# A softmax kernel's stores move from ACT's hardware DMA queue to Pool's software queue

## The chip, the cores and the metric

The kernel runs on one core of a Trainium2 chip. Five of its parts appear below: DVE (VectorE), ACT (ScalarE) and Pool (GpSimd) compute, SP (SyncE) here only issues transfers and waits, and 16 DMA engines move the data. A transfer is issued by an instruction on a queue; it has landed when its semaphore (the counter on which the engine waits) lets the waiting engine go on. "The last load landed" is read from the start of the DVE operation that waited for it. The metric is device time in microseconds (us) of one execution. The span in a profile runs from the first to the last instruction of the program and is about 1.8 us shorter than the device time (before: 316.0 against 317.86 us in the profiled execution).

## The reference

```python
def setup_inputs():
    batch, seq, dim = 32, 512, 1024
    return {"x": np.random.randn(batch, seq, dim).astype(np.float32), "temperature": 0.5}

def reference(x, temperature):
    scaled = x / temperature
    shifted = scaled - np.max(scaled, axis=-1, keepdims=True)
    exp_x = np.exp(shifted)
    return (exp_x / np.sum(exp_x, axis=-1, keepdims=True)).astype(np.float32)
```

That is 16384 rows of 1024 floats: 67.11 MB are read and 67.11 MB written.

## The kernel before

The rows are cut into 16 tiles of 128 partitions with 8 rows each (4 MB a tile, 32 KB a partition, in one piece in DRAM and in SBUF). Six tile buffers are in use. SP issues the loads. A tile is worked on in two groups of four rows: DVE takes the maximum, ACT the exponential with its sum, DVE divides in place. When both groups of a tile are divided, ACT issues the store, and the load into that buffer waits for the store to land.

```python
TILES = [[8]] * 16
BUFS = 6
GROUP = 4
# ... (cut)
    def load():
        i = len(tiles)
        if i < len(TILES):
            xt = data.tile([P, sum(TILES[i]), d], f32, name="xt")
            nc.sync.dma_start(out=xt, in_=dram(xf, i))
            tiles.append(xt)
# ... maximum(g): tensor_reduce over four rows, then bias = -scale * top; exponential(g): four activations (cut)
    def divide(g):
        # ... (cut)
        nc.vector.reciprocal(recip, sums)
        for b in range(k):
            nc.vector.tensor_scalar_mul(
                tiles[i][:, a + b, :], in0=tiles[i][:, a + b, :], scalar1=recip[:, b : b + 1]
            )

    def store(g):
        i, _, _, part = groups[g]
        if part:
            a, k = part
            nc.scalar.dma_start(out=dram(of, i)[:, a : a + k, :], in_=tiles[i][:, a : a + k, :])
            if a + k == sum(TILES[i]):
                load()

    with tc.manual_schedule():
        for _ in range(BUFS):
            load()
        for g in range(len(groups) + 1):
            if g < len(groups):
                maximum(g)
                exponential(g)
            if g > 0:
                divide(g - 1)
                store(g - 1)
```

In the profile, L61 is the load, L70 the maximum, L79 the exponential, L91 the reciprocal, L93 the divide, L101 the store and L147 the program's end.

## Time and profile before

| | before |
|---|---|
| time, median | 318.11 us (3 runs, 318.0 to 318.13) |
| DVE, ACT, Pool busy | 75%, 47%, 0% |
| bytes, mean rate over the span | 134.25 MB, 425 GB/s |
| store: issue to landing, median | 38.6 us |
| load: issue to landing, median | 50.2 us |

These lines are from the page of the kernel before: busy time by engine; the DMA queues (packets, MB, share of the 16 engines' span); three groups of instructions (after the bar: busy us and mean ns of one, then the idle time before them and what ended it); and the DMA issues (size, median us to landing).

```profile
DVE 235.5 (75%) x224; ACT 149.6 (47%) x257; POOL 0.2 (0%) x4
...
q1 hardware_dynamic: 2304, 67.11, 49.7%
q10 hardware_dynamic: 2304, 67.11, 49.2%
...
L79 ACT ACTIVATE xt<-xt,bias 128x1024 f32<-128x1024 f32 x128 | 145.4, 1137 | 136.8 <-DVE recip L91 119.4
L70 DVE TENSOR_REDUCE top<-xt 128x4 f32<-128x4096 f32 x32 | 141.3, 4416 | 62.6 <-DMA xt<-in_x_dram 62.6
L93 DVE TENSOR_SCALAR xt<-xt,recip 128x1024 f32<-128x1024 f32 x128 | 87.7, 749 | 1.1
...
xt<-in_x_dram SPq DMA_DIRECT2D x16, 4096.0 KB, 50.2
out_dram<-xt ACTq DMA_DIRECT2D x16, 4096.0 KB, 38.6
```

The two queues together hold the engines for 98.9% of the span. Two rows of the table of windows (stretch, its length, busy us by engine, clock, DMA share, GB/s) show the steady part:

```profile
core 0: us, DVE busy (x) ACT busy (x) POOL busy (x), PEclk, DMA share, GB/s
...
80.00:120.00 40.00, 31.40 (x32) 18.96 (x33) 0.00 (x0) 1.00 1.00 433
...
240.00:280.00 40.00, 29.46 (x28) 19.44 (x34) 0.00 (x0) 1.00 1.00 433
```

A DMA share of 1.00 at 433 GB/s means that there is nothing to gain in the steady part from starting a transfer earlier, and nothing to lose from starting it a little later while others are queued (delay_all below, with every store held up: 1.0018 of this kernel's time). The packet records say how much later: from the fourth store to the thirteenth, a store's first packet starts 18.1 to 19.0 us after its issue, about when the store before it has finished. So a store's start has some 18 us of room there. The last store has little: its first packet starts 1.0 us after its issue. This is the timeline of the tail (start us, duration us, engine, line, operation):

```profile
282.62 4.42 DVE L70 TENSOR_REDUCE top<-xt 128x4 f32<-128x4096 f32 x1 [4.50 <-DMA xt<-in_x_dram]
...
290.13 0.34 ACTq L101 DMA_DIRECT2D out_dram<-xt  x1
...
299.61 2.74 DVE L93 TENSOR_SCALAR xt<-xt,recip 128x1024 f32<-128x1024 f32 x4
302.38 0.34 ACTq L101 DMA_DIRECT2D out_dram<-xt  x1
```

The last load has landed at 282.62 us, and the last store is issued 19.8 us later.

### The profile page before, as it was taken

The numbers are of one execution on the slowest core, as the hardware profiler recorded it, in microseconds if no ns is written. First come the engines' busy times: TensorE is split into PE (matmuls) and PEld (weight loads), VectorE is DVE, ScalarE is ACT, GpSimd is POOL, SyncE is SP. The second block draws the span as 40 slices with busy tenths as digits, with TensorE's granted clock in tenths as the row PEclk, the third lists the DMA queues.
The fourth block names the chain that finished last, engine by engine and source line by source line (L and its number), as shares of the span: only waits on it lengthen the run. The fifth ranks groups of instructions, "written<-read, shape, count | busy, mean of one in ns | idle before, by whom it ended". The sixth has DMA issues, their size and how long they took to land.

```text
span 316.0 us, 620 instructions
## 1 busy us (share of the span) xinstructions
DVE 235.5 (75%) x224; ACT 149.6 (47%) x257; POOL 0.2 (0%) x4
## 2 busy tenths in 40 slices
DVE  0399999999689494994949859497693976949720
ACT  0176666666526255361554605546064560645500
POOL 0000000000000000000000000000000000000000
DMA  8999999999999999999999999999999999999996
GB/s 332 411 452 423 373 460 415 452 425 431 436 427 440 427 444 423 444 419 448 415 452 411 452 408 456 423 444 427 436 431 432 440 423 444 419 444 419 452 411 274
DMA packets 4612, 134.25 MB, mean 425 GB/s; under 512 B 512, under 2 KB 512, under 8 KB 512
## 3 DMA queue, kind: packets, MB, share of 16 engines
q1 hardware_dynamic: 2304, 67.11, 49.7%
q10 hardware_dynamic: 2304, 67.11, 49.2%
q14 instruction: 4, 0.03, 0.0%
HBM read 67.11 MB, written 67.11 MB: 425 GB/s over the span
## 4 chain that ended last, share of the span: by engine, by line
DVE 49%; DMA 32%; another core or an unknown queue 9%; ACT 5%; issue 1%; DVEq 0%; SPq 0%
DVE top L70 29%; DMA xt<-in_x_dram 20%; DVE xt L93 18%; DMA out_dram<-xt 12%; ACT xt L79 5%; DVE recip L91 1%; DVE bias L73 1%; DVEq L147 0%; SPq L61 0%
## 5 line engine op out<-in xcount | busy, mean ns | idle before, releaser
L79 ACT ACTIVATE xt<-xt,bias 128x1024 f32<-128x1024 f32 x128 | 145.4, 1137 | 136.8 <-DVE recip L91 119.4
L70 DVE TENSOR_REDUCE top<-xt 128x4 f32<-128x4096 f32 x32 | 141.3, 4416 | 62.6 <-DMA xt<-in_x_dram 62.6
L93 DVE TENSOR_SCALAR xt<-xt,recip 128x1024 f32<-128x1024 f32 x128 | 87.7, 749 | 1.1
L79 ACT ACTIVATION_READ_ACCUMULATOR xt<-xt,bias 128x1 f32 x128 | 23.9, 187 | 0.0
L79 ACT ACT_TABLE_LOAD x1 | 1.3, 1283 | 13.0 <-DMA xt<-in_x_dram 13.0
L91 DVE RECIPROCAL recip<-sums 128x4 f32<-128x4 f32 x32 | 5.5, 171 | 2.1 <-ACT xt L79 2.1
L73 DVE TENSOR_SCALAR bias<-top 128x4 f32<-128x4 f32 x32 | 5.4, 170 | 1.1
L133 POOL MEMSET const-bfloat16-1.0<- 128x1 bf16 x1 | 0.1, 101 | 0.0
L133 POOL MEMSET const-uint8-127<- 128x1 uint8 x1 | 0.1, 101 | 0.0
L133 POOL MEMSET const-float32-0.0<- 128x1 f32 x1 | 0.1, 98 | 0.2 <-issue 0.2
L133 POOL MEMSET const-float32-1.0<- 128x1 f32 x1 | 0.1, 98 | 0.0
## 6 DMA issues: line engine op xcount, KB each, us to landing
xt<-in_x_dram SPq DMA_DIRECT2D x16, 4096.0 KB, 50.2
out_dram<-xt ACTq DMA_DIRECT2D x16, 4096.0 KB, 38.6
```

The lines of the kernel that those rows point to most:

```text
L70: nc.vector.tensor_reduce(out=top, in_=tiles[i][:, a : a + k, :], axis=mybir.AxisListType.X, op=extreme)
L73: nc.vector.tensor_scalar_mul(bias, in0=top, scalar1=-scale)
L79: nc.scalar.activation(tiles[i][:, a + b, :], tiles[i][:, a + b, :], mybir.ActivationFunctionType.Exp, bias=bias[:, b : b + 1], scale=scal ...
L91: nc.vector.reciprocal(recip, sums)
L93: nc.vector.tensor_scalar_mul(tiles[i][:, a + b, :], in0=tiles[i][:, a + b, :], scalar1=recip[:, b : b + 1])
L133: nc = _bacc.Bacc("TRN2", target_bir_lowering=False, num_devices=1)
```

## The change

The intent: take the stores off ACT's queue and give them to Pool, which has nothing else to do, so that ACT only computes. The price is that Pool's stores go through a software queue (q0, software_dynamic on the page after); what this adds before a store's first packet I could only estimate.

```diff
         if part:
             a, k = part
-            nc.scalar.dma_start(out=dram(of, i)[:, a : a + k, :], in_=tiles[i][:, a : a + k, :])
+            nc.gpsimd.dma_start(out=dram(of, i)[:, a : a + k, :], in_=tiles[i][:, a : a + k, :])
             if a + k == sum(TILES[i]):
                 load()
```

## The prediction

> **What bounds the kernel now.** The 16 DMA engines. The page counts 134.25 MB at a mean 425 GB/s; a table of 40 us windows shows DMA share 1.00 and 431 to 433 GB/s from 40 to 280 us. 134.2 MB at 433 GB/s is 310 us of the 316.0 us span; the rest is start and end (data stops near 313.2 us). DVE is busy 75%, ACT 47%; the waits of DVE (62.6 us on loads) and of ACT (119.4 us) are slack. The chain of waits (49% DVE) misleads: in the steady part every DVE stretch follows a wait for a load.
>
> **What the change moves.** Sixteen 4096 KB stores leave ACT's queue for Pool's; bytes and the work of DVE and ACT are the same. Removed: 16 issues of 0.34 us from ACT's queue. In the timeline a store already issues 0.12 us after its last divide, between exponentials, and ACT waits for DVE anyway. Gain: 0.
>
> [...] But each store comes just after the four divides (2.74 us); then DVE runs a 4.41 us reduce[...], so I expect each store to start 1 to 3 us later at most. In the steady part this costs nothing: stores take 38.6 us to land at a 19.3 us period, so two are in flight, with two or three loads (50.2 us).
>
> **Where it can show: the tail.** The last load lands at 282.6 us. Its compute takes 19.8 us; the last store issues at 302.38. From 282.6 the engines still have about 13.2 MB (30.5 us) to move, so without the last store they would run dry about 1 us after its issue. Two outcomes:
>
> - Shares stay equal (or loads get more): the last store's later start shows, +0.5 to 2.5 us. About 319 to 320.5 us.
> - Stores get a larger share. [...] If a software store's descriptors form one packet per engine, each store (9.7 us alone at 433 GB/s) passes the loads, landing in 10 to 20 us. Stores then no longer queue; the last load lands later, at about 291 us, and the 19.8 us of compute plus a 9.7 us store stand behind it, with the engines idle about 10 us. Estimate: span about 325, time 324 to 328 us.
>
> No trace here shows the software queue's packets; I give the first outcome about 62%, the second 36%.
>
> **Prediction:** 320.5 us, range 317.6 to 328. Faster by over 2%: 0.01; within 2%: 0.65; slower: 0.34.
>
> **What would show it.** Right: DVE and ACT busy and means unchanged (TENSOR_REDUCE 4414, TENSOR_SCALAR 749 ns); the store's queue listed as software, same 67.11 MB; 433 GB/s in 40 to 280 us. First outcome: median store landing stays near 38 us, last load near 283 us. Second: store landing 10 to 20 us, load landing above 55 us, last reduce-wait ending near 290 us, holes in the DMA row in the last three slices.
>
> **What would make it wrong.** Packets in the thousands and a steady rate under 425 GB/s[...]: over 328. [...] A start or end cost of the software queue outside the span. Faster than 317 only if the rate rises above 433 GB/s.

## The result, and the profile after

| | before | after |
|---|---|---|
| time, median | 318.08 us (4 runs, 318.0 to 318.13) | 318.28 us (4 runs, 318.17 to 318.68) |
| ratio | | 1.0009, 95% interval 0.9991 to 1.0026: the same |
| store: issue to landing, median | 38.6 us | 38.4 us |
| last load landed, profiled execution | 282.62 us | 282.87 us |

Ratios here are the mean time of one kernel's fast runs over that of the other's in the same rounds, so they are not quite the ratio of the medians quoted.

From the page of the kernel after; Pool's store instruction is now counted as work of Pool:

```profile
DVE 235.5 (74%) x224; ACT 149.6 (47%) x257; POOL 8.8 (3%) x20
...
q1 hardware_dynamic: 2304, 67.11, 49.5%
q0 software_dynamic: 2304, 67.11, 49.1%
...
issue 89%; DMA 4%; POOL 2%; POOLq 0%
...
L70 DVE TENSOR_REDUCE top<-xt 128x4 f32<-128x4096 f32 x32 | 141.3, 4416 | 62.8 <-DMA xt<-in_x_dram 62.8
L93 DVE TENSOR_SCALAR xt<-xt,recip 128x1024 f32<-128x1024 f32 x128 | 87.7, 749 | 1.1
...
L101 POOL DMA_DIRECT2D out_dram<-xt x16 | 8.6, 540 | 294.4 <-DVE xt L93 294.4
...
xt<-in_x_dram SPq DMA_DIRECT2D x16, 4096.0 KB, 50.2
out_dram<-xt POOLq DMA_DIRECT2D x16, 4096.0 KB, 38.4
```

Three readings. First, the software queue has the same 2304 packets as the hardware queue (16 stores of 128 data packets and 16 closing ones). Second, DVE's and ACT's durations have not moved. Third, the chain of waits is of no use here: it followed Pool's own queue back and calls 89% of the span "issue" (time in which the engine waited for nothing that the profile shows). The steady part, in the same two windows:

```profile
80.00:120.00 40.00, 31.14 (x31) 18.56 (x33) 1.06 (x2) 1.00 1.00 433
...
240.00:280.00 40.00, 29.46 (x28) 19.03 (x33) 1.06 (x2) 1.00 1.00 433
```

The tail of the kernel after, as a timeline:

```profile
282.87 4.42 DVE L70 TENSOR_REDUCE top<-xt 128x4 f32<-128x4096 f32 x1 [4.48 <-DMA xt<-in_x_dram]
...
290.65 0.53 POOL L101 DMA_DIRECT2D out_dram<-xt  x1 [18.82 <-DVE xt L93]
...
299.86 2.74 DVE L93 TENSOR_SCALAR xt<-xt,recip 128x1024 f32<-128x1024 f32 x4
302.90 0.53 POOL L101 DMA_DIRECT2D out_dram<-xt  x1 [11.72 <-DVE xt L93]
```

The last divide ends at 302.60 us and Pool begins 0.30 us later; before, the last divide ended at 302.35 us and ACT issued 0.03 us later. So the issue is 0.27 us later. (My texts say 0.12 and 0.38 us; there I had counted from the start of the next DVE operation, which overlaps the divide's end. The difference is the same.) Pool's store instruction takes 0.53 us, ACT's issue took 0.34 us.

One thing did get longer, at the very end. These rows list the semaphore instructions of SP's queue on the program's last line, in the kernel before and then in the kernel after (count, duration ns, first and last start us):

```profile
L147 SPq EVENT_SEMAPHORE  x7: 17/28/28, 270.5 to 315.9; - x7
```

```profile
L147 SPq EVENT_SEMAPHORE  x11: 17/28/28, 315.5 to 316.8; - x11
```

Before the program ends, SP goes through a list of waits for DMA semaphores: five wait instructions before the change, nine after it (the other two instructions of each row come later). Single times here are from the trace's records. In the kernel before, the earlier stores' waits are done while the last store is still moving; the last of them passes at 315.20 us and SP goes on at 315.26 us. In the kernel after, the first wait in SP's list passes only at 315.46 us, when the last store has landed, and eight more wait instructions, by then fulfilled, follow at 0.06 us each, so SP goes on at 316.01 us. The order of the list costs here as much as its length: the wait that passes last stood at its end before and stands at its head now. From the last data packet to the span's end it is 1.19 us before and 1.85 us after.

### The profile page after: what moved, and what is told of

The parts are those of the page before. It is cut to its first block, busy times and chain, and to the rows that moved or that the text cites. A ratio compares the mean times of both kernels' runs of the same rounds, so it can differ in the third digit from the quotient of the medians.

```text
span 316.9 us, 639 instructions
## 1 busy us (share of the span) xinstructions
DVE 235.5 (74%) x224; ACT 149.6 (47%) x257; POOL 8.8 (3%) x20
## 3 DMA queue, kind: packets, MB, share of 16 engines
q1 hardware_dynamic: 2304, 67.11, 49.5%
q0 software_dynamic: 2304, 67.11, 49.1%
## 4 chain that ended last, share of the span: by engine, by line
issue 89%; DMA 4%; POOL 2%; POOLq 0%
DMA xt<-in_x_dram 4%; POOL out_dram L101 2%; POOLq L147 0%; POOLq L101 0%
## 5 line engine op out<-in xcount | busy, mean ns | idle before, releaser
L70 DVE TENSOR_REDUCE top<-xt 128x4 f32<-128x4096 f32 x32 | 141.3, 4416 | 62.8 <-DMA xt<-in_x_dram 62.8
L101 POOL DMA_DIRECT2D out_dram<-xt x16 | 8.6, 540 | 294.4 <-DVE xt L93 294.4
## 6 DMA issues: line engine op xcount, KB each, us to landing
out_dram<-xt POOLq DMA_DIRECT2D x16, 4096.0 KB, 38.4
```

The source lines that it names most:

```text
L70: nc.vector.tensor_reduce(out=top, in_=tiles[i][:, a : a + k, :], axis=mybir.AxisListType.X, op=extreme)
L101: nc.gpsimd.dma_start(out=dram(of, i)[:, a : a + k, :], in_=tiles[i][:, a : a + k, :])
```

## The experiments

Sixteen kernels were run. Times of the kernel before in the same rounds had medians of 317.90 to 318.06 us.

### What a store's later start costs when nothing hides it: b2_act and b2_pool

With two buffers, every load waits for a store, so a store's start is in the time.

```diff
-BUFS = 6
+BUFS = 2
```

> Two tile buffers instead of six, stores from ACT: each load waits for a store to land, so every microsecond of a store's start is in the time. Estimate about 500 us (16 periods of about 31.5 us: 7.5 us of compute, a store and a load of about 12 us each when alone). It is the control for b2_pool.

> Two tile buffers, stores from Pool. Theory A (a software store starts only some tenths of a us later, as the issue at +0.38 us after the divides against +0.12 us shows): 2 to 6 us longer than b2_act over 14 to 16 exposed stores. Theory B (my prediction's term: 1 to 3 us later start per store, which six buffers only hid): 14 to 45 us longer. Theory C (no cost at all): within 1 us.

Measured: 494.75 us (494.52 to 495.0) from ACT, 501.80 us (501.77 to 502.29) from Pool; both correct. Time from issue to landing, minimum/median/maximum, from ACT and then from Pool:

```profile
DMA to landing us min/median/max: 11.1/11.1/12.1
```

```profile
DMA to landing us min/median/max: 11.3/11.4/12.3
```

The last load's data ended at 460.34 us with ACT and at 467.35 us with Pool. Fourteen loads had waited for a store by then, so a software store costs 0.50 us each (7.01 us over 14): 0.27 us of it a later issue after the divide, 0.2 to 0.3 us more from issue to landing. The packet records agree: the first packet starts 0.84 us after the issuing instruction's start on ACT and 1.10 us on Pool. (The 0.50 us is from one trace of each. By the median times, less about 0.5 us of longer end, it is 0.4 to 0.5 us.) That is just above what theory A expected for the total (2 to 6 us, measured 7.05) and far below theory B, the 1 to 3 us of the prediction. Theory C falls too: the cost is real, and six buffers hide it.

### Holding the stores up on purpose: delay_all, delay_but_last, delay_last, delay_last_double

Pool first copies 3072 elements per partition of the tile, which takes 2.75 us, and then issues the store.

```diff
             a, k = part
+            if True:                       # delay_all
+            # delay_but_last: if i < len(TILES) - 1;  delay_last: if i == len(TILES) - 1
+                pause = spare.tile([P, 3, d], f32, name="pause")
+                nc.gpsimd.tensor_copy(out=pause, in_=tiles[i][:, 5:8, :])   # twice in delay_last_double
             nc.gpsimd.dma_start(out=dram(of, i)[:, a : a + k, :], in_=tiles[i][:, a : a + k, :])
```

(One comparison stands in each kernel; `spare` is a pool with one buffer.)

> Six buffers, stores from Pool, and Pool first copies 3072 elements per partition, so that each store is issued a few us later (D, read from the issue times; I guess 3 to 5 us). Theory A (steady part has slack for it, the last store has under 1 us): time is that of the changed kernel plus D minus 0 to 1 us. Theory of no tail exposure: within 0.5 us of the changed kernel. Theory of exposure at every store: over 10 us longer.

> As delay_all, but the last store is issued without the copy. Theory A: within 0.6 us of the changed kernel (318.3 us), although 15 of 16 stores start D later. If the steady part has no slack: as long as delay_all or longer than it.

Measured: delay_all 318.55 us (318.47 to 318.84; ratio to the kernel before 1.0018, 95% interval 1.0005 to 1.003), delay_but_last 318.40 us (318.29 to 319.8; ratio 1.0011, 0.9997 to 1.0025). I had expected delay_all to be longer by the delay less at most 1 us. It was not, and the timeline of its tail shows why:

```profile
278.94 4.42 DVE L71 TENSOR_REDUCE top<-xt 128x4 f32<-128x4096 f32 x1 [4.42 <-DMA xt<-in_x_dram]
...
298.79 2.75 POOL L104 COPY pause<-xt 128x3072 f32<-128x3072 f32 x1 [9.03 <-issue]
301.48 0.53 POOL L105 DMA_DIRECT2D out_dram<-xt  x1
```

The last load now lands at 278.94 us, 3.9 us earlier than in the kernel after (and earlier than in any execution that does not delay the earlier stores, where it lies between 281.0 and 282.9 us). The DMA share is 1.00 from 40 to 280 us here too, so what the stores don't use while they are held up goes to the loads; they run ahead, and the last tile's compute begins sooner. A delay that is the same for every store shifts the last load as well and is paid back in the tail.

The long run of delay_but_last (319.8 us, its profiled one) had a data end 12.8 us after the last store's first packet where the others have 9.9 to 11.4 us. The packet records show that 15 engines end by 313.87 us, and one at 316.02 us; what made this one late I don't know. Its other four runs lie between 318.29 and 318.51 us.

So the last store was held up alone:

> Only the last store is issued later, by Pool's copy of 2.7 us (2.3 us later than in the changed kernel). Theory A2 (delay_all cost only about 0.2 us because delaying the earlier stores brings the last load forward, by 3.9 us in its trace; the tail itself has under 1 us of slack): here the last load still lands near 282.9 us, the last store issues near 305.2 us, the engines run dry for 1 to 2 us, and the time is 319.5 to 320.6 us. Rival (the tail simply has 3 us or more of slack): within 0.4 us of delay_all, 318.6 us.

Measured: 318.36 us, with runs from 318.04 to 320.0 us. By its median this missed the expectation, and for a reason that I had not allowed for: in the profiled execution (318.19 us) the last load landed at 281.11 us and not near 282.9 us. Was that chance, or does the tail have more slack than I thought?

> The changed kernel once more, unchanged. If the last load's landing varies from one execution to the next: it is not at 282.9 us but anywhere from 281 to 284 us, with a span of 316.2 to 317 us. If it belongs to the program: 282.7 to 283.1 us.

> As same1: a third trace of the same program, with the same two readings (landing anywhere from 281 to 284 us, or 282.7 to 283.1 us).

> delay_last unchanged. If the landing varies by execution: last load anywhere from 281 to 284 us, the last store's first packet 23.6 us after it, and data ends at the later of about 314.8 us and that packet plus 9.9 us. If it belongs to the program: 281.1 us again, span 316.4 us.

> Only the last store is held up, by two copies (about 5.4 us). By the traces so far data ends at the later of about 314.8 us and the last store's first packet plus 9.9 us. First packet 26.3 us after the last load lands (281 to 283 us), so at 307.3 to 309.3 us: data ends at 317.2 to 319.2 us, time 320.8 to 322.8 us. If the tail has much more slack: within 0.5 us of delay_last, 318.4 us.

Measured: same1 and same2, the changed kernel unaltered, took 318.15 and 318.53 us, with the last load landing at 281.14 and 281.64 us. The landing varies by almost 2 us from one execution to the next (282.87 us in the first trace). The chip is not the reason: the four programs of this call are alike up to the last store, ran on one chip, and their last loads landed between 281.00 and 282.70 us. delay_last_again took 319.77 us; its last load landed at 282.70 us. These are the ends of delay_last and of delay_last_again:

```profile
281.11 4.42 DVE L71 TENSOR_REDUCE top<-xt 128x4 f32<-128x4096 f32 x1 [4.50 <-DMA xt<-in_x_dram]
...
303.59 0.53 POOL L105 DMA_DIRECT2D out_dram<-xt  x1
```

```profile
282.70 4.42 DVE L71 TENSOR_REDUCE top<-xt 128x4 f32<-128x4096 f32 x1 [4.49 <-DMA xt<-in_x_dram]
...
305.18 0.53 POOL L105 DMA_DIRECT2D out_dram<-xt  x1
```

It is the same program twice (on two chips), with the last issue 1.6 us apart and the time 1.6 us apart. The expectation of delay_last_again had stated what was to happen if the landing varied: first packet 23.6 us after the landing, which is 306.3 us, and data end 9.9 us later, 316.2 us. Measured: 306.27 and 316.18 us. delay_last_double took 321.24 us (320.87 to 321.48): with the last store held up by 5.5 us the cost appears, in the range that was expected (320.8 to 322.8 us). Its last load landed at 281.00 us, as early as in delay_last:

```profile
300.79 5.55 POOL L105 COPY pause<-xt 128x3072 f32<-128x3072 f32 x2 [11.49 <-DVE xt L94]
306.28 0.53 POOL L106 DMA_DIRECT2D out_dram<-xt  x1
```

### Does the divide lock Pool out: busy_scale_pool, busy_max_pool, busy_scale_act

In the changed kernel DVE runs a tensor_reduce after the divides, and Pool's store instruction runs beside it. Here another DVE operation is put right behind the divides that a store waits for: a tensor_scalar, which by the lock theory (a supposition of mine that no trace had shown by then) holds Pool up, and as a control a tensor_reduce, which by that theory does not.

```diff
             nc.gpsimd.dma_start(...)              # nc.scalar in busy_scale_act
+            extra = spare.tile([P, 3, d], f32, name="extra")
+            nc.vector.tensor_scalar_mul(extra, in0=tiles[i][:, 5:8, :], scalar1=2.0)
+            # busy_max_pool: nc.vector.tensor_reduce(out=extra[:, :, 0], in_=tiles[i][:, 5:8, :], ..., op=extreme)
```

> Right after the divides that a store waits for, the vector engine runs one more tensor_scalar over 3072 elements (about 2.2 us[...]). Lock theory: Pool's store instruction, 0.53 us before, lasts or starts until that operation ends, so 1.8 to 2.5 us, and stores start about 2 us later. No-lock theory: 0.53 us and issued 0.38 us after the divides as before. Time in either case 318 to 321 us, so this is read from the instruction's duration and start.

> Control for busy_scale_pool: the added operation is a tensor_reduce over the same 3072 elements (about 3.3 us)[...]. Lock theory and no-lock theory alike: Pool's instruction stays at 0.53 us.

> The same added tensor_scalar with the stores on ACT: a hardware-queue store is not held up, issue 0.34 us, 0.12 us after the divides. Its time tells what the added 2.2 us of vector work costs by itself; busy_scale_pool minus this is what the lock costs: lock theory 0 to 2 us, no-lock theory 0 to 0.4 us.

Measured: 318.65 us (318.36 to 318.8), 319.63 us (319.38 to 320.75) and 317.75 us (317.57 to 318.15). The timeline of one store in busy_scale_pool and then in busy_max_pool:

```profile
302.87 1.76 DVE L104 TENSOR_SCALAR extra<-xt 128x3072 f32<-128x3072 f32 x1
303.13 1.62 POOL L102 DMA_DIRECT2D out_dram<-xt  x1 [12.43 <-DVE xt L94]
```

```profile
305.90 3.35 DVE L104 TENSOR_REDUCE extra<-xt 128x3 f32<-128x3072 f32 x1
306.16 0.53 POOL L102 DMA_DIRECT2D out_dram<-xt  x1 [15.10 <-DVE xt L94]
```

The same place in busy_scale_act, where ACT issues the store:

```profile
303.79 0.34 ACTq L102 DMA_DIRECT2D out_dram<-xt  x1
303.79 1.76 DVE L104 TENSOR_SCALAR extra<-xt 128x3072 f32<-128x3072 f32 x1
```

Beside the tensor_scalar, Pool's store instruction lasts 1.62 us in place of 0.53 us and ends at 304.75 us, 0.12 us after DVE's operation ends (304.63 us). All 16 stores of that run take 1.60 to 1.62 us. Beside the tensor_reduce, though it is longer, Pool keeps its 0.53 us (median of 16). Beside the same tensor_scalar, ACT's issue in busy_scale_act keeps its 0.34 us. The lock theory holds for these two operations. My expected 1.8 to 2.5 us was too long only because the added operation took 1.76 us, not 2.2 us. In the changed kernel a reduce stands behind the divides, and Pool's store instruction takes 0.53 us: the lock costs nothing there. Even in busy_scale_pool it cost only 0.90 us against busy_scale_act, part of that being the longer end.

### Who gets the engines when packets differ: l4_act, l4_pool, s4_act, s4_pool

My second outcome needed stores to take a larger share than loads. The packet counts had already said that the two queues' packets are alike (2304 each), so here they are made unlike.

```diff
-        return block.rearrange("(p k) d -> p k d", p=P, k=k)
+        if small:
+            return block.rearrange("(k p) d -> p k d", p=P, k=k)     # runs of 4 KB
+        return block.rearrange("(p k) d -> p k d", p=P, k=k)         # runs of 32 KB
```

`small` is a new argument of `dram`, False unless given. In l4_* the loads use small runs (`dram(xf, i, small=True)`), in s4_* the stores.

> Wrong output on purpose (rows permuted): loads read 4 KB rows apart from each other, so they are cut into runs of 4 KB, stores stay at 32 KB, both from hardware queues. Packet theory (queues alternate packet by packet, so larger packets get the larger share, 8 to 1): stores land in 10 to 20 us instead of 38.6, the last load lands near 290 us, engines have holes in the tail, time 324 to 330 us if 4 KB packets run at full rate. Byte-fair theory: stores land in about 38 us, last load near 283 us, time near 318 us or longer by what small packets cost in the steady part.

> As l4_act with the stores from Pool. If the software queue is treated by the engines as a hardware queue is: within 1% of l4_act and the same store landing within 1 us. If the software queue groups its descriptors or has another share: store landing differs by over 3 us.

> Wrong output on purpose (rows permuted): stores are cut into runs of 4 KB, loads stay at 32 KB. Packet theory: stores get a ninth of the engines while loads are waiting, so stores land later than 38.6 us (45 us or more) and the last load lands before 275 us; no hole in the tail, so the time is that of the kernel before plus what small packets cost. Byte-fair theory: landing near 38 us.

> As s4_act with the stores from Pool, which now has 1024 data descriptors per store in place of 128. If writing them is what Pool's 0.53 us consists of, the instruction takes 3 to 5 us (0.53 times up to 8), and the divides can hold it up (over 6 us for some); if 0.53 us is a fixed cost, it stays under 1 us. Time: within 1% of s4_act in either case, as the start of a store is hidden by the queue.

| kernel | time, us | store landing, us | load landing, us | last load's data ends, us |
|---|---|---|---|---|
| l4_act | 337.39 (337.26 to 337.58) | 15.4 | 53.9 | 303.29 |
| l4_pool | 339.22 (338.45 to 339.46) | 15.7 | 54.4 | 304.46 |
| s4_act | 324.32 (324.13 to 324.42) | 52.3 | 16.4 | 267.30 |
| s4_pool | 327.53 (326.23 to 327.82) | 58.4 | 18.0 | 271.11 |

In these four runs the larger packets get the larger share, whichever direction they go: the stores of l4_act and l4_pool land in 15.4 and 15.7 us, the loads of s4_act and s4_pool in 16.4 and 18.0 us. With large store packets the tail is what the prediction's second outcome described. From the table of windows of l4_act:

```profile
core 0: us, DVE busy (x) ACT busy (x) POOL busy (x), PEclk, DMA share, GB/s
...
300.00:305.00 5.00, 1.28 (x1) 0.00 (x0) 0.00 (x0) 1.00 0.16 66
305.00:310.00 5.00, 4.93 (x6) 1.57 (x3) 0.00 (x0) 1.00 0.00 0
310.00:315.00 5.00, 5.00 (x3) 3.06 (x6) 0.00 (x0) 1.00 0.74 315
```

The engines stand idle for some ten microseconds while the last tile is computed. So the mechanism was right, and it is longer than I had estimated (19 us over the kernel before, where 6 to 12 us were expected; the last load's wait ended at 303.7 us, where about 290 us were expected; part of it is the steady rate of about 420 GB/s with small packets). The share is 8 to 1, although the landing of 15.4 us (11.1 us alone) does not look like it. In l4_act's packet records, while a store's packets move, the engines spend 0.88 of their time on 32 KB store packets and 0.12 on 4 KB load packets, and start about as many of one kind as of the other (the fifth to the fourteenth store: 112 store packets and 103 to 108 load packets up to the point where the store's first engines finish). Where no other transfer is left, a store needs 9.90 us from first packet to last; here it needs 11.0 to 11.8 us in most stores (eight packets of 1.213 us per engine with a load packet of 0.16 us beside each make 10.98 us). The rest of the 15.4 us is the first packet, 3.5 us after the issue where it is 0.84 us alone; why it waits there was not tested.

The software queue behaves as the hardware queue does: the same landing within 0.3 us in l4, and the time 0.5% longer. In s4_pool, where each store is 1024 data packets, it is 1.0% slower than s4_act, at the edge of what I had expected, with 6.1 us later landing; I did not follow this further. The issue instructions, in s4_act and then in s4_pool (duration ns minimum/median/maximum):

```profile
L103 ACTq DMA_DIRECT2D out_dram<-xt x16: 378/11797/18479, 32.7 to 303.3; - x16
```

```profile
L103 POOL DMA_DIRECT2D out_dram<-xt x16: 877/879/1013, 33.0 to 292.0; - x16
```

Eight times the data packets lengthen Pool's instruction from 0.53 to 0.88 us only, so most of the 0.53 us is fixed. ACT's issue instruction, on the other hand, lasts 11.8 us per store (median) in s4_act, against 0.34 us with 128 data packets per store; what prolongs it I did not test.

### The tail's law

Moments in us from the span's start, worked out from the packet records of each profiled execution:

```
                    last load   store before it,    last store's   last data   last data less
kernel              landed      last engine ends    first packet   ends        first packet
before              282.62      305.11              303.39         314.80      11.41
after               282.87      305.37              304.01         315.06      11.05
same1               281.14      304.87              303.43         314.56      11.13
same2               281.64      305.25              303.63         314.94      11.31
delay_all           278.94      305.09              303.43         314.77      11.34
delay_but_last      280.19      306.34              303.26         316.02      12.76
busy_scale_act      282.23      304.74              304.63         314.53       9.90
delay_last          281.11      304.84              304.69         314.60       9.91
busy_scale_pool     281.31      305.06              305.32         315.23       9.91
delay_last_again    282.70      305.20              306.27         316.18       9.90
busy_max_pool       282.76      305.26              307.26         317.18       9.91
delay_last_double   281.00      304.72              307.38         317.29       9.90
```

A 4 MB store alone needs 9.90 us for its packets, and eight data packets of 32 KB on one engine, at 1.213 us each, need 9.70 us. With these two numbers the end of the data is, to 0.02 us, the later of two moments in all twelve rows: the last store's first packet plus 9.90 us, or the moment at which the last engine is done with the store before (its closing packet) plus 9.70 us. In the first six rows the second moment decides, and the last store's start is not in the time at all; from busy_scale_act on the first decides. This also says where the long run of delay_but_last comes from: one engine was done with the store before only at 306.34 us.

An early start does not help because the engines do not finish together: in the kernel before, 14 engines close the last store between 313.0 and 313.8 us and the other two at 314.4 and 314.8 us, while in delay_last all 16 close within 0.2 us. (Idle time per engine from 308 us to the end of the data: 1.3 us before, 0.07 us in delay_last.) A start that is later by up to about one packet takes away only this unevenness. The kernel before had 1.5 us of room (305.11 plus 9.70, less 9.90 and 303.39), the kernel after 1.2 us.

## Why the prediction was right or wrong

- **What bounds the kernel: right.** DMA share 1.00 and 433 GB/s in the same windows before and after; freeing ACT's queue brought nothing. That a later start costs nothing in the steady part was right too: a store's first packet waits about 18 us there anyway.
- **DVE and ACT unchanged, a reduce behind the divides: right.** 4416 and 749 ns both times. That Pool's store instruction is not held up beside a reduce (0.53 us) but is beside a tensor_scalar (1.62 us) was shown only by busy_max_pool and busy_scale_pool.
- **"within 2%" and the range: right** (318.28 us lies in 317.6 to 328, near the lower end), **but the 2.4 us that were forecast are not there.** Measured: +0.20 us of the medians, interval -0.3 to +0.8 us (0.9991 to 1.0026 of 318 us).
- **The term that was mis-sized: "I expect each store to start 1 to 3 us later at most".** A software store costs 0.50 us, where nothing hides it (b2_pool against b2_act). The first packet starts 0.26 us later from the issuing instruction's start, 0.5 us later from the end of the divide. The 1 to 3 us were my estimate; no trace that I had showed such a delay.
- **The step that failed: "the last store's later start shows, +0.5 to 2.5 us".** I had found that the engines "would run dry about 1 us after its issue", and subtracted none of it from the delay. Measured, the last store's first packet had 1.5 us of room. A start that is about 0.5 us later, within 1.5 us of room, costs nothing that the times resolve. Beyond the room the cost is 1 us for 1 us (busy_scale_pool and the three rows after it in the tail's table). And a delay of every store by 2.5 us is hardly seen in the tail, since the loads run ahead meanwhile (delay_all: 0.27 us over the changed kernel, by medians).
- **The second outcome at 36%: wrong premise.** "If a software store's descriptors form one packet per engine": the software queue shows 2304 packets, as the hardware queue does, and the landing stayed at 38.4 us. The consequence that I drew from unequal shares, until then an estimate, was right in kind (l4_act, where the larger packets have 0.88 of the engines' time), but it does not apply. A third of the probability, and with it part of the 2.4 us, rested on it.
- **"A start or end cost of the software queue outside the span"** was named as a risk. There is an end cost, inside the span: SP's eight further semaphore waits, 0.5 us after the last store has landed. The end is longer in every kernel with Pool's stores (last data packet to end of span 1.71 to 1.85 us in the Pool kernels, 1.15 to 1.27 us in the ACT kernels). It can account for the +0.20 us in full. That it does is not shown by time, since 0.5 us is within the spread of executions; the waits themselves are in the trace.

## What to carry to other kernels

Which engine issued the stores mattered little here (ratio 1.0009), because the 16 engines are the bound (DMA share 1.00) and several transfers are queued: look at the DMA share and at the queue depth (time to landing over period, here 38.6 over 19.3 us) first. When you cost a delay, subtract the slack at the place where it would show, and ask whether the same delay also moves what comes before it. If a software queue is used, mind which DVE operation runs beside Pool's store instruction (here 0.53 us beside a tensor_reduce, 1.62 us beside a tensor_scalar), and compare the packet sizes of the queues that share the engines (in l4_act 32 KB packets had 0.88 of the engines' time beside 4 KB packets).
